# Operand stores on the GpSimd queue, operands made one by one behind weight chunks, and shared loads in the feed-forward part of a transformer block

## Chip, cores and metric

One core of one Trainium2 chip. The metric is the device time of one execution in microseconds (us), lower is better. The kernel before takes 2645.63 us, the median of three runs (2642.18 to 2647.23).

## What is computed

One layer over 512 tokens with 2048 channels, all in float32. The change lies in its second half:

```
z = rms_norm(x) @ w_in                       # then a state-space branch and an attention branch
m = sigmoid(g_s) * (y_ssm @ w_proj_ssm) + sigmoid(g_a) * (y_attn @ w_proj_attn)
x = x + m @ w_out
h = rms_norm(x)
x = x + (silu(h @ w_ffn_gate) * (h @ w_ffn_up)) @ w_ffn_down      # 2048 -> 5632 -> 2048
```

## The kernel before

**Products in float32.** A weight chunk is 128x2x512 (256 rows of the matrix by 512 columns, 512 KB). `split` (L460) makes two parts of it: ScalarE rounds it (`whi`, L461), VectorE takes the rest (`wlo = x - whi`, L462). With an operand that was split in the same way, TensorE does three matmuls: hi by hi, hi by lo, lo by hi. There are three buffers each for `whi` and `wlo`. `linear` (L453) does all matrices up to w_out so.

**The feed-forward part** (`ffn`) uses seven products of half matrices in place of eight. `seven` (L1008 issues its matmuls) goes through the products in the order 1, 2, 7, 5, 6, 3, 4 (in the first unit 1, 7, 2, 5, 6, 3, 4). Each takes its weights chunk by chunk from `weights(i, c)`, then `done(i, banks)` takes the result from PSUM. After each chunk one entry of a list `fill` is run, if any is left.

**Gate and up**: eleven units u = 0 to 10 of 512 hidden columns; in each every product has 4 chunks and 48 matmuls. `weights` sums blocks of the matrices on VectorE (`add`, L1037): A is a slab of 8x512 that goes from w11 to w11-w12 (product 7), then plus w22 (6); product 7 loads two chunks and sums them, 6 and 3 load w22 one after the other, and for product 4 w21 is added to A by an accumulating load on GpSimd's queue (L1108). Raw chunks lie in three buffers and a few places of a slab E.

**Operands of the down product.** When unit u runs, the activations of unit u - 1 are transposed (`flip_act`: four flips of four transposes on TensorE, L1027, evacuated to E by ScalarE, L1060), one behind each chunk of product 2. Behind flip 2 operands 1 and 7 are made, behind flip 4 the other five, each bunch at once: sums on VectorE (L958, L966 to L968), a `split` into two tiles `wk` (L461, L462), and two stores of 256 KB to a buffer `opd` in DRAM on SP's queue (L1066). The pool `wk` has five buffers of 128x512; two of them hold the gate's values from product 1 until product 3 has been evacuated. For unit 0 the operands come out of w_out's result and stay in SBUF; their sums run on GpSimd, in w_out and in unit 0.

**Down**: blocks of units [0], [1, 2], ... [9, 10], each for v = 0 and 1 (two halves of the output). Block 0 has one chunk per product, the others two. Operands come back from `opd` (L1182), product 4 uses an accumulating load again (L1206), and sums stay in SBUF (`done`, L1215 on ScalarE in block 0). The operands of unit 10 are made in block 0, v = 0.

**The end**: `final` (L1155 and on) flips four results, adds x2 (loaded from DRAM to a `wk` tile on ScalarE's queue, L1162) and stores 256 KB (SP, L1164). Eight finals of v = 0 and four of v = 1 are filled into the last block, the last four stand behind it.

**What sets the order.** TensorE's order in `ffn` is that of the program. The other engines' instructions are placed by a scheduler that works from priorities and an estimate of time; each engine then runs its instructions in that fixed order, and one that waits holds all behind it.

Of the kernel before, what the change touches and what calls it, by code (L numbers as in the profile page):

```python
# [12 lines left out]
ALU = mybir.AluOpType  # L13
# [18 lines left out]
class Block:  # L32
# [427 lines left out]
    def split(self, hi, lo, x):  # L460
        self.nc.scalar.activation(hi, x, AF.Copy)  # L461
        self.nc.vector.tensor_tensor(lo, x, hi.bitcast(F32), op=ALU.subtract)  # L462

# [257 lines left out]
    def build(self, out):  # L721
# [226 lines left out]
    ORDER = (1, 2, 7, 5, 6, 3, 4)  # L948
# [32 lines left out]
    def seven(self, n, weights, ops, done, order=ORDER, fill=()):  # L981
# [7 lines left out]
        for i in order:  # L989
            if i in (1, 7):  # L990
                banks[i] = [self.bank("lin") for _ in range(2)]
            elif i in (2, 5):
                banks[i] = [self.bank("S") for _ in range(2)]
            else:
                banks[i] = banks[{6: 1, 3: 5, 4: 7}[i]]
            for c in range(0, n, 2):
                raw = weights(i, c)

                self.nc3 = (self.nc3 + 1) % 3
                hi, lo = (self.wp.tile([P, 2, T], F32R, tag=t, name=self.uid(t)) if self.nc3 else  # L1000
                          self.fp.tile([P, 2, T], F32R, tag=t, name=self.uid(t)) for t in ("whi", "wlo"))
                self.split(hi, lo, raw)
                for kk in range(2):
                    k = c + kk
                    for tt in range(2):
                        xh, xl = (ops[i][:, h, k, tt * P:(tt + 1) * P] for h in range(2))
                        for q, (l, r) in enumerate(((xh, hi), (xh, lo), (xl, hi))):
                            nc.tensor.matmul(banks[i][tt], l, r[:, kk, :], start=(i in (1, 7, 2, 5) and k == 0 and q == 0),  # L1008
                                             stop=(k == n - 1 and q == 2), skip_group_check=True)
                if i != order[0] and fill:  # L1010
                    fill.pop(0)()
            done(i, banks[i])
        assert not fill

# [15 lines left out]
    def ffn(self, ops, steps, x2d, out):  # L1030
# [25 lines left out]
        def flip_act(u, j):  # L1056

            x1, x2 = self.E[:, 4:6], self.E[:, 6:8]
            tp = self.flips([act[u, tt][:, j * P:(j + 1) * P] for tt in range(4)])
            nc.scalar.activation((x1, x2)[j // 2][:, j % 2], tp, AF.Copy)  # L1060
# [7 lines left out]
            if j == 1:  # L1068
                self.operands_1(put, x1, lambda: self.work((P, 2, 256)), dve)
            elif j == 3:  # L1070
                step = self.operands_2(put, x1, x2, dve)
                for i in (2, 5, 6, 3, 4):
                    step(i, 0, True, True)

        flips_act = lambda u: [lambda j=j: flip_act(u, j) for j in range(4)] if u >= 0 else []

        for u in range(NU):
# [4 lines left out]
            def weights(i, c):  # L1082
                for _ in range(2 if i == 7 else 1):
                    if steps:
                        steps.pop(0)()
# [7 lines left out]
                if i in (2, 3):  # L1093
                    return load(raw(), b(2, 1) if i == 2 else b(2, 2))
                if i == 7:
                    r1, r2 = load(raw(), b(1, 2)), load(raw(), b(2, 2))
                    if not first:
                        add(dve, A, A, r1)
                    add(dve, r2, r1, r2)
# [5 lines left out]
                elif i == 6:  # L1105
                    add(dve, A, A, load(raw(), b(2, 2)))
# [40 lines left out]
            order = (1, 7, 2, 5, 6, 3, 4) if first else self.ORDER  # L1147
            self.seven(8, weights, ops, done, order, flips_act(u - 1))
# [7 lines left out]
        def final(v, m, j):  # L1156
# [4 lines left out]
            o = self.work()  # L1161
            nc.scalar.dma_start(o, x2d[t])  # L1162
# [9 lines left out]
        for b, units in enumerate(blocks):  # L1172
# [7 lines left out]
            for i in self.ORDER:  # L1180
                for c, u in enumerate(units):
                    nc.sync.dma_start(ops[i][:, :, 2 * c:2 * c + 2].bitcast(F32), opd[u, i - 1])  # L1182
            for v in range(2):

                o = 2 * v if b == 0 else 0

                def weights(i, c, A=A[:, o:], R=R[:, o:], Q=Q[:, o:]):
# [45 lines left out]
                self.seven(n, weights, ops, done, self.ORDER, fill)  # L1233
                if b or v:
# [41 lines left out]
```

## Time and profile before

| | |
|---|---|
| median of 3 runs | 2645.63 us |
| the profiled execution, and its span | 2639.38 us, 2637.5 us |
| TensorE busy | 2554.5 us (97%) |
| VectorE, ScalarE, GpSimd busy | 2053.7 (78%), 1176.5 (45%), 383.4 us (15%) |
| DMA | 474.28 MB, mean 180 GB/s |
| first matmul of the feed-forward part | at 1280.6 us |
| last matmul of it | ends at 2625.9 us |

Busy time of TensorE counts matmuls at the pace that its clock allowed: after a long wait matmuls are slower and count as busy all the same. So a stage is best read by its length beside that of the same work elsewhere.

### The profile page before, as it was taken

To read this page: it belongs to the slowest core of one execution; us is meant where nothing else is said; L and a number is where in the kernel's file an instruction comes from. 1 tells how busy PE (TensorE), PEld (TensorE's weight loads), DVE (VectorE), ACT (ScalarE), POOL (GpSimd) and SP (SyncE) were. 2 spreads that over 40 slices of the span, in tenths; PEclk is the share of its full clock that TensorE was granted. 3 is DMA by queue.
4 is the path that set the end of the run, shared out by engine and by line. 5 is a ranking of instruction groups with operands and counts; after the bars stand their busy time and mean duration, and the time that the engine had idled before them with its cause. 6 is when DMAs were issued, how large, how long until landed. Compare 5 with 4: busy or idle time off the path is not lost.

```text
span 2637.5 us, 32145 instructions
## 1 busy us (share of the span) xinstructions
PE 2554.5 (97%) x11351; PEld 2043.4 (77%) x11351; DVE 2053.7 (78%) x3345; ACT 1176.5 (45%) x1783; POOL 383.4 (15%) x472
## 2 busy tenths in 40 slices
PE   7999999999999999999999999999999998999998
PEld 5777777777787777888777878887887876888887
DVE  8799999999557865525678887778877786788888
ACT  4244444444255643224444545545545445333332
POOL 5232232221011100015300000000000000000000
PEclk9999999999999999999999999999999998999999
DMA  5444344434443434433668777778777798667774
GB/s 156 144 117 116 113 118 120 122 112 104 124 148 120 133 104 160 156 113 127 200 199 270 220 227 221 221 229 264 218 228 218 230 301 293 188 214 234 242 232 139
DMA packets 243329, 474.28 MB, mean 180 GB/s; under 512 B 22472, under 2 KB 22536, under 8 KB 243168
## 3 DMA queue, kind: packets, MB, share of 16 engines
q1 hardware_dynamic: 201248, 386.98, 45.3%
q0 software_dynamic: 37408, 81.02, 13.4%
q10 hardware_dynamic: 4512, 4.24, 0.6%
q8 instruction: 89, 1.46, 0.2%
q14 instruction: 72, 0.59, 0.1%
HBM read 401.35 MB, written 65.03 MB: 177 GB/s over the span
## 4 chain that ended last, share of the span: by engine, by line
issue 47%; PE 32%; DVE 13%; DMA 3%; POOL 3%; ACT 1%; SPq 0%; DVEq 0%; POOLq 0%; ACTq 0%
PE lin L453 25%; PE lin L1008 3%; PE S L1008 2%; DVE wlo L432 2%; POOL s L1108 2%; DVE c L363 1%; DMA s<-in_w_ffn_down_dram 1%; DVE s L364 1%; PE O L413 1%; DMA bi<-in_ssm_b_im_dram 1%; DVE t L400 1%; DVE wlo L462 1%; DVE t L395 1%; DVE s L1037 1%; POOL s L1206 1%
## 5 line engine op out<-in xcount | busy, mean ns | idle before, releaser
L453 PE MATMUL lin<-s,whi 128*128 128x512 f32 x2432 | 738.6, 396 | 1.6 <-DVE s L462 1.0
L1008 PE MATMUL lin<-whi,s 128*128 128x512 f32 x2112 | 669.8, 393 | 10.0 <-ACT whi L461 10.0
L461 ACT ACTIVATE whi<-s 128x1024 fp32r<-128x1024 f32 x354 | 372.9, 1059 | 459.2 <-PE lin L1008 231.7
L462 DVE TENSOR_TENSOR wlo<-s,whi 128x1024 fp32r<-128x1024 f32 x354 | 431.7, 1223 | 180.4 <-ACT whi L461 179.5
L453 PEld LDWEIGHTS lin<-s,whi 128*128 128x128 f32 x2432 | 453.4, 189 | 124.6 <-issue 22.3
L1008 PE MATMUL S<-whi,s 128*128 128x512 f32 x1584 | 510.0, 393 | 4.0 <-DVE wk L1037 3.4
L1008 PEld LDWEIGHTS lin<-whi,s 128*128 128x128 f32 x2112 | 399.8, 189 | 93.9 <-ACT whi L461 11.3
L453 PE MATMUL lin<-s,wlo 128*128 128x512 f32 x1216 | 448.0, 395 | 12.2 <-DVE wlo L432 12.2
L1008 PE MATMUL lin<-wlo,s 128*128 128x512 f32 x1056 | 417.0, 395 | 22.2 <-DVE wlo L462 22.0
L432 DVE TENSOR_TENSOR wlo<-raw,whi 128x1024 fp32r<-128x1024 f32 (+1 forms) x201 | 252.2, 1255 | 175.3 <-ACT whi L431 168.9
L431 ACT ACTIVATE whi<-raw 128x1024 fp32r<-128x1024 f32 (+1 forms) x201 | 211.3, 1052 | 330.6 <-PE lin L453 283.0
L1008 PEld LDWEIGHTS S<-whi,s 128*128 128x128 f32 x1584 | 298.2, 188 | 66.5 <-ACT whi L461 4.8
L1008 PE MATMUL S<-wlo,s 128*128 128x512 f32 x792 | 309.7, 391 | 4.3 <-DVE wlo L462 4.2
L453 PEld LDWEIGHTS lin<-s,wlo 128*128 128x128 f32 x1216 | 229.8, 190 | 65.9 <-DVE wlo L432 15.5
L1008 PEld LDWEIGHTS lin<-wlo,s 128*128 128x128 f32 x1056 | 200.0, 189 | 74.2 <-DVE wlo L462 33.4
L453 PE MATMUL lin<-whi,s 128*128 128x512 f32 x768 | 245.6, 394 | 0.0
L1008 PEld LDWEIGHTS S<-wlo,s 128*128 128x128 f32 x792 | 149.1, 188 | 36.8 <-DVE wlo L462 6.7
L453 PEld LDWEIGHTS lin<-whi,s 128*128 128x128 f32 x768 | 144.0, 188 | 38.8 <-issue 7.2
L1108 POOL DMA_DIRECT2D s<-in_w_ffn_gate_dram x44 | 53.3, 1223 | 783.7 <-DVE wlo L462 754.6
L462 DVE TENSOR_TENSOR wlo<-raw,whi 128x1024 fp32r<-128x1024 f32 x103 | 125.8, 1225 | 42.5 <-ACT whi L461 42.5
L461 ACT ACTIVATE whi<-raw 128x1024 fp32r<-128x1024 f32 x103 | 108.8, 1057 | 105.8 <-PE S L1008 42.0
L453 PE MATMUL lin<-wlo,s 128*128 128x512 f32 x384 | 150.1, 391 | 2.7 <-DVE wlo L432 2.7
(346 smaller groups left out, 2734.4 us busy)
## 6 DMA issues: line engine op xcount, KB each, us to landing
raw<-in_w_in_dram SPq DMA_DIRECT2D x127, 512.0 KB, 3.8
raw<-in_w_ffn_up_dram SPq DMA_DIRECT2D x115, 512.0 KB, 4.8
opd<-wk SPq DMA_DIRECT2D x154, 256.0 KB, 4.7
s<-opd SPq DMA_DIRECT2D x77, 512.0 KB, 9.0
s<-in_w_ffn_down_dram SPq DMA_DIRECT2D x66, 512.0 KB, 5.8
s<-in_w_ffn_gate_dram SPq DMA_DIRECT2D x64, 512.0 KB, 5.5
s<-in_w_ffn_up_dram SPq DMA_DIRECT2D x60, 512.0 KB, 4.7
s<-in_w_ffn_gate_dram POOLq DMA_DIRECT2D x44, 512.0 KB, 10.5
```

What stands on the lines that cost most here:

```text
L363: nc.vector.scalar_tensor_tensor(c[:, hi], s[:, lo], nps[:, j:j + 1], c[:, hi], op0=ALU.mult, op1=ALU.add)
L364: nc.vector.scalar_tensor_tensor(s[:, hi], c[:, lo], ps[:, j:j + 1], s[:, hi], op0=ALU.mult, op1=ALU.add)
L395: nc.vector.tensor_tensor_scan(t1, mag, t1, 0.0, op0=ALU.mult, op1=ALU.add)
L400: nc.vector.tensor_tensor_scan(t3, mag, t3, 0.0, op0=ALU.mult, op1=ALU.add)
L413: nc.tensor.matmul(y[32 * q:32 * q + 32, :], CT[:, ri, 32 * q:32 * q + 32], states[q][ri], start=(ri == 0), stop=(ri == 1))
L431: nc.scalar.activation(hi[:, ks], raw[:, ks], AF.Copy)
L432: nc.vector.tensor_tensor(lo[:, ks], raw[:, ks], hi[:, ks].bitcast(F32), op=ALU.subtract)
L453: nc.tensor.matmul(acc[b], l, r, start=(k == 0 and i == 0), stop=(k == nk - 1 and i == 2))
L461: self.nc.scalar.activation(hi, x, AF.Copy)
L462: self.nc.vector.tensor_tensor(lo, x, hi.bitcast(F32), op=ALU.subtract)
L1008: nc.tensor.matmul(banks[i][tt], l, r[:, kk, :], start=(i in (1, 7, 2, 5) and k == 0 and q == 0), stop=(k == n - 1 and q == 2), skip_group ...
L1108: pool.dma_start(A, two(b(2, 1)), accum_op=ALU.add)
```

## The change

- Sums of operands of unit 0: from GpSimd to VectorE.
- The order has a group (6, 3): chunk by chunk first 6, then 3, both with one load of w22. Both are evacuated when both are done; product 5, whose banks 3 goes on with, is evacuated before.
- Operands of unit u - 1: flips behind the chunks of product 2 as before, five empty entries, and then one operand each behind chunks 2, 3 and 4 of product 5 and chunks 1 and 2 of 6 and 3. `behind` ties each to the chunk split that goes ahead of it. Sums are made in place. Stores go to GpSimd's queue.
- Block 0 has places of its own for weights, and its product 4 adds on VectorE. Unit 10's operands are spread over both v of block 0.
- x2 of the last eight finals comes by one load of 2 MB into a slab, issued when product 7 of the last v is done.
- In product 7 the sum for r2 comes ahead of that for A; in the first unit the two steps at a time are popped in product 2 in place of 7.

```diff
-        step = self.operands_2(put, x2[0], x2[1], nc.gpsimd)
+        step = self.operands_2(put, x2[0], x2[1], nc.vector)
...
-                    self.operands_1(put, x2[0], lambda: self.work((P, 2, 256)), nc.gpsimd)
+                    self.operands_1(put, x2[0], lambda: self.work((P, 2, 256)), nc.vector)
...
-    ORDER = (1, 2, 7, 5, 6, 3, 4)
+    ORDER = (1, 2, 7, 5, (6, 3), 4)
...
             for c in range(0, n, 2):
-                raw = weights(i, c)
+                for i in group:
+                    raw = weights(i, c)
...
+                    self.last = self.split(hi, lo, raw)
...
+                    if i == group[-1] and c == n - 2:
+                        for j in group:
+                            done(j, banks[j])
+                    if i != order[0] and fill:
+                        fill.pop(0)()
...
+    def behind(self, ins):
+
+        self.tc.add_manual_dep(ins.ins, self.last.ins.name, mybir.DependencyInfo(
+            mybir.DependencyClass.NoSync, mybir.DependencyReason.DATA), reason="order")
...
-            def put(i, k, x):
-                hl = [self.work((P, 2, 256), F32R) for _ in range(2)]
-                self.split(*hl, x)
-                for h in range(2):
-                    nc.sync.dma_start(opd[u, i - 1, :, h], hl[h].bitcast(F32))
...
+            def step(i, x, op=None):
+                def f():
+                    if op:
+                        self.behind(op())
+                    hl = [self.work((P, 2, 256), F32R) for _ in range(2)]
+                    self.behind(self.split(*hl, x))
+                    for h in range(2):
+                        pool.dma_start(opd[u, i - 1, :, h], hl[h].bitcast(F32))
+                return f
...
+            return [step(1, x11), step(2, x12),
+                    step(7, x11, lambda: add(dve, x11, x11, x21, ALU.subtract)),
+                    step(5, x21, lambda: add(dve, x21, x21, x22, ALU.subtract)),
+                    step(6, x11, lambda: dve.scalar_tensor_tensor(x11, x11, -1.0, x22, op0=ALU.mult, op1=ALU.subtract)),
+                    step(3, x12, lambda: add(dve, x12, x12, x11)),
+                    step(4, x22)]
...
-                for _ in range(2 if i == 7 else 1):
+                for _ in range(2 if i == 2 else 1):
...
+                if i == 3:
+                    return st["w22"]
                 if i == 7:
                     r1, r2 = load(raw(), b(1, 2)), load(raw(), b(2, 2))
+                    add(dve, r2, r1, r2)
                     if not first:
                         add(dve, A, A, r1)
-                    add(dve, r2, r1, r2)
...
                 elif i == 6:
-                    add(dve, A, A, load(raw(), b(2, 2)))
+                    st["w22"] = load(raw(), b(2, 2))
+                    add(dve, A, A, st["w22"])
...
-            self.seven(8, weights, ops, done, order, flips_act(u - 1))
+            self.seven(8, weights, ops, done, order, flips_act(u - 1) + [lambda: None] * 5 + make(u - 1) if u else ())
...
-            o = self.work()
-            nc.scalar.dma_start(o, x2d[t])
+            if v:
+                o = st["x2"][:, t - 8]
+            else:
+                o = self.work()
+                nc.scalar.dma_start(o, x2d[t])
...
+                    own = self.A[:, 6 * v:], raw() if v else self.A[:, 2:], self.A[:, 4:]
...
                     if i == 4:
-                        pool.dma_start(A, two(blk(2, 1)), accum_op=ALU.add)
+                        if n == 2:
+                            add(dve, A, A, R)
+                        else:
+                            pool.dma_start(A, two(blk(2, 1)), accum_op=ALU.add)
...
+                    if last and v and i == 7:
+
+                        st["x2"] = self.slab("s7", (P, 8, T), F32)
+                        nc.sync.dma_start(st["x2"], x2d[8:16].rearrange("k p t -> p k t"))
...
                 if b == 0 and v == 0:
-                    fill = both(flips_act(NU - 1))
+                    made = make(NU - 1)
+                    fill = both(flips_act(NU - 1)) + made[:4]
+                elif b == 0:
+                    fill = made[4:]
```

How this moves instructions shows at three places. In the names, `s_1872` is A; E is `s_1899` before and `s_1907` after; `lin` and `S` are PSUM banks.

**VectorE in product 7 of unit 1, before.** L1037 are sums of weights or evacuations, L958, L966 and L967 sums of operands, `wk` the low halves of operands.

```order
L462 TENSOR_TENSOR wlo_11957<-raw_11952,whi_11956 128x1024
L1037 TENSOR_TENSOR wk_11777<-wk_11777,S_11781 128x512
L1037 TENSOR_TENSOR s_1872_11382<-s_1872_11382,s_1899_11549 128x1024
L1037 TENSOR_TENSOR s_1899_11549<-s_1899_11549 128x1024
L1037 TENSOR_TENSOR wk_11779<-wk_11779,S_11782 128x512
L462 TENSOR_TENSOR wlo_11979<-raw_11974,whi_11978 128x1024
L966 TENSOR_TENSOR s_1899_11549<-s_1899_11549 128x2x256
L462 TENSOR_TENSOR wk_11838<-wk_11835,wk_11837 128x512
L462 TENSOR_TENSOR wlo_11999<-s_1899_11549,whi_11998 128x1024
L967 TENSOR_TENSOR s_1899_11549<-s_1899_11549 128x2x256
L462 TENSOR_TENSOR wlo_12017<-s_1872_11382,whi_12016 128x1024
```

**VectorE from the end of product 7 of unit 1 on, after the change.** The first row splits the last chunk of product 7, the next the first chunk of 5.

```order
L462 TENSOR_TENSOR wlo_11946<-raw_11941,whi_11945 128x1024
L462 TENSOR_TENSOR wlo_11964<-s_1872_11382,whi_11963 128x1024
L1048 TENSOR_TENSOR s_1872_11382<-s_1872_11382,raw_12052 128x1024
L462 TENSOR_TENSOR wlo_11980<-s_1872_11382,whi_11979 128x1024
L462 TENSOR_TENSOR wk_11996<-s_1907_11613,wk_11995 128x512
L1048 TENSOR_TENSOR s_1872_11382<-s_1872_11382,raw_12101 128x1024
L462 TENSOR_TENSOR wlo_12002<-s_1872_11382,whi_12001 128x1024
L462 TENSOR_TENSOR wk_12018<-s_1907_11613,wk_12017 128x512
L1048 TENSOR_TENSOR s_1907_11613<-s_1907_11613 128x2x256
L1048 TENSOR_TENSOR s_1872_11382<-s_1872_11382,s_1907_11613 128x1024
L462 TENSOR_TENSOR wlo_12024<-s_1872_11382,whi_12023 128x1024
L462 TENSOR_TENSOR wk_12047<-s_1907_11613,wk_12046 128x512
```

Operand work is no longer between the splits of product 7; a half (later with a sum ahead of it) now stands behind each split of 5, 6 and 3.

**SP's queue in unit 1, before**, where stores of operands stand among the loads of weights:

```order
L1066 DMA opd<-wk_11892 128x512
L1066 DMA opd<-wk_11898 128x512
L1053 DMA raw_12184<-in_w_ffn_up_dram 128x2x512
L1066 DMA opd<-wk_11905 128x512
L1066 DMA opd<-wk_11899 128x512
L1053 DMA raw_12202<-in_w_ffn_up_dram 128x2x512
L1066 DMA opd<-wk_11912 128x512
L1066 DMA opd<-wk_11906 128x512
```

**GpSimd's queue in unit 1, after the change** (L1086 are the stores, L1132 the accumulating loads of product 4; before, those loads stood alone here):

```order
L1086 DMA opd<-wk_12072 128x512
L1132 DMA s_1872_11382<-in_w_ffn_gate_dram 128x2x512
L1086 DMA opd<-wk_12073 128x512
L1086 DMA opd<-wk_12095 128x512
L1086 DMA opd<-wk_12096 128x512
L1086 DMA opd<-wk_12121 128x512
L1132 DMA s_1872_11382<-in_w_ffn_gate_dram 128x2x512
L1086 DMA opd<-wk_12122 128x512
L1086 DMA opd<-wk_12143 128x512
L1132 DMA s_1872_11382<-in_w_ffn_gate_dram 128x2x512
L1086 DMA opd<-wk_12144 128x512
L1132 DMA s_1872_11382<-in_w_ffn_gate_dram 128x2x512
```

The stores of 154 tiles leave SP's queue, and four of a unit's stores now follow its first accumulating load.

**VectorE in block 0, v = 0, after the change**, from the split for product 5 (first row) over those for 6 and 3 to the one for product 4 (last row):

```order
L462 TENSOR_TENSOR wlo_17844<-s_1872_11382,whi_17843 128x1024
L1048 TENSOR_TENSOR s_1872_11382<-s_1872_11382 128x1024
L462 TENSOR_TENSOR wk_17862<-s_1907_11613,wk_17861 128x512
L1048 TENSOR_TENSOR s_1907_11613<-s_1907_11613 128x2x256
L462 TENSOR_TENSOR wlo_17869<-s_1872_11382,whi_17868 128x1024
L1048 TENSOR_TENSOR s_1872_11382<-s_1872_11382 128x1024
L462 TENSOR_TENSOR wlo_17893<-s_1872_11382,whi_17892 128x1024
L1048 TENSOR_TENSOR s_1907_11613<-s_1907_11613 128x2x256
L462 TENSOR_TENSOR wk_17887<-s_1907_11613,wk_17886 128x512
L462 TENSOR_TENSOR wlo_17919<-s_1872_11382,whi_17918 128x1024
```

The sixth row is the sum that takes the place of the accumulating load, ahead of the splits for products 3 and 4; halves and sums of unit 10's operands (`wk`, `s_1907`) stand between them.

## Rows read from the trace of the kernel before

**Rows 1.** The page's first part: busy us, share of the span and number of instructions of each engine.

```profile
PE 2554.5 (97%) x11351; PEld 2043.4 (77%) x11351; DVE 2053.7 (78%) x3345; ACT 1176.5 (45%) x1783; POOL 383.4 (15%) x472
```

**Rows 2.** The view of the waits of TensorE over the whole span: what waited, for what, us in total, times, longest.

```profile
PE lin L1008 <- DVE wlo L462: 22.0, 21, 3.4
...
PE lin L1008 <- ACT whi L461: 10.0, 3, 5.8
...
PE S L1008 <- DVE wk L1037: 3.4, 1, 3.4
```

**Rows 3.** Windows of the span: start and end in us, length, busy us (and instructions) of TensorE, its weight loads, VectorE, ScalarE and GpSimd, granted clock, share of the DMA engines, GB/s. In order: 66 us of w_out; unit 0; units 1 to 10; of unit 2 products 2, 7, 6 and 4; of unit 10 product 3; block 0 with v = 0 and v = 1; from the last product's end to the span's end.

```profile
1188.00:1254.00 66.00, 66.00 (x293) 54.66 (x292) 39.45 (x28) 27.60 (x37) 34.44 (x26) 1.00 0.39 125
1280.60:1372.20 91.60, 81.70 (x345) 65.88 (x344) 73.54 (x83) 46.62 (x59) 23.73 (x18) 0.96 0.81 250
1372.20:2173.50 801.30, 786.62 (x3521) 644.85 (x3521) 628.07 (x651) 408.64 (x490) 48.42 (x40) 1.00 0.78 234
1463.50:1476.20 12.70, 12.70 (x66) 10.47 (x64) 11.06 (x11) 6.90 (x10) 0.00 (x0) 1.00 0.78 236
1476.20:1488.40 12.20, 11.40 (x52) 9.07 (x50) 10.92 (x13) 7.00 (x9) 0.00 (x0) 1.00 0.90 300
1499.20:1510.70 11.50, 11.19 (x50) 8.93 (x48) 9.45 (x10) 6.57 (x9) 4.85 (x4) 1.00 1.06 264
1521.60:1532.50 10.90, 10.90 (x50) 9.03 (x49) 8.57 (x10) 4.25 (x4) 0.00 (x0) 1.00 0.61 203
2147.60:2160.50 12.90, 11.52 (x50) 9.02 (x49) 5.94 (x7) 6.36 (x8) 0.00 (x0) 1.00 1.06 309
2173.50:2201.20 27.70, 23.98 (x102) 19.09 (x101) 21.41 (x26) 18.94 (x30) 1.20 (x1) 0.89 0.61 184
2201.20:2231.90 30.70, 22.84 (x85) 17.52 (x84) 17.68 (x17) 14.33 (x20) 1.20 (x1) 0.83 1.03 352
2626.00:2637.50 11.50, 3.33 (x24) 2.25 (x22) 4.52 (x7) 0.00 (x0) 0.00 (x0) 0.75 0.60 205
```

**Rows 4.** Timeline of VectorE in product 7 of unit 2: start in us, us, engine, line, operation, output and inputs, then the idle time before it and what ended it.

```profile
1478.80 1.23 DVE L1037 TENSOR_TENSOR s<-s,s 128x1024 f32<-128x1024 f32 x1 [1.28 <-DMA s<-in_w_ffn_up_dram]
...
1481.67 1.22 DVE L462 TENSOR_TENSOR wlo<-raw,whi 128x1024 fp32r<-128x1024 f32 x1
1482.81 0.69 DVE L966 TENSOR_TENSOR s<-s 128x512 f32<-128x512 f32 x1
1483.41 0.69 DVE L462 TENSOR_TENSOR wk<-wk,wk 128x512 fp32r<-128x512 f32 x1
1484.01 1.22 DVE L462 TENSOR_TENSOR wlo<-s,whi 128x1024 fp32r<-128x1024 f32 x1
```

**Rows 5.** Timeline of ScalarE shortly after.

```profile
1489.00 0.64 ACT L461 ACTIVATE wk<-s 128x512 fp32r<-128x512 f32 x1 [2.12 <-DMA opd<-wk]
```

**Rows 6.** The view of the tensor opd: who waited for it (us, times).

```profile
  ACT wk L461: 55.6, 29
```

**Rows 7.** The view of the DMA issues by group: names, queue, count, KB each, median us from issue to landing.

```profile
opd<-wk SPq DMA_DIRECT2D x154, 256.0 KB, 4.7
...
s<-in_w_ffn_gate_dram POOLq DMA_DIRECT2D x44, 512.0 KB, 10.5
...
x2d<-s POOLq DMA_DIRECT2D x16, 256.0 KB, 2.5
...
out_dram<-wk SPq DMA_DIRECT2D x16, 256.0 KB, 2.7
```

**Rows 8.** Groups of GpSimd's instructions by line: count, busy us, mean ns of one.

```profile
L966 POOL TENSOR_TENSOR s<-s,s 128x512 f32<-128x512 f32 x4 | 7.0, 1754 | 4.6 <-ACT s L909 4.6
```

**Rows 9.** Timeline of VectorE in unit 0.

```profile
1292.54 1.75 DVE L462 TENSOR_TENSOR s<-s,s 128x512 fp32r<-128x512 f32 x1
...
1295.35 2.28 DVE L462 TENSOR_TENSOR wlo<-ring,whi 128x1024 fp32r<-128x1024 f32 x1
```

**Rows 10.** Timeline of TensorE in unit 0, the first matmul after a wait and one 3.07 us later.

```profile
1297.69 0.79 PE L1008 MATMUL lin<-wlo,s 128*128 128x512 f32 x1 [3.37 <-DVE wlo L462]
...
1300.76 0.63 PE L1008 MATMUL lin<-whi,s 128*128 128x512 f32 x2
```

**Rows 11.** Timeline of ScalarE in block 0.

```profile
2193.94 1.06 ACT L461 ACTIVATE whi<-s 128x1024 fp32r<-128x1024 f32 x1 [4.88 <-DMA s<-in_w_ffn_down_dram]
...
2210.75 1.06 ACT L461 ACTIVATE whi<-s 128x1024 fp32r<-128x1024 f32 x1 [3.87 <-DMA wk<-x2d]
...
2224.68 2.00 ACT L461 ACTIVATE whi<-s 128x1024 fp32r<-128x1024 f32 x2 [3.16 <-DMA s<-in_w_ffn_down_dram]
```

**Rows 12.** Timeline of TensorE in block 0.

```profile
2195.05 0.79 PE L1008 MATMUL lin<-whi,s 128*128 128x512 f32 x1 [3.25 <-ACT whi L461]
...
2225.79 0.79 PE L1008 MATMUL lin<-whi,s 128*128 128x512 f32 x1 [5.85 <-ACT whi L461]
...
2227.64 1.05 PE L1008 MATMUL lin<-whi,s 128*128 128x512 f32 x2
...
2228.92 1.05 PE L1008 MATMUL lin<-whi,s 128*128 128x512 f32 x2
```

**Rows 13.** Timeline of VectorE at the end.

```profile
2633.72 0.69 DVE L1037 TENSOR_TENSOR wk<-wk,T 128x512 f32<-128x512 f32 x1 [3.58 <-DMA wk<-x2d]
```

**Rows 14.** The view of line L1108, the accumulating loads of the units.

```profile
DMA to landing us min/median/max: 6.7/10.5/16.1
```

More of the change, by code (lines that the diff above doesn't have):

```diff
@@ L988, in seven @@
         fill = list(fill)
[L989 to L995, printed above, removed]
-            for c in range(0, n, 2):
-                raw = weights(i, c)
[L999 to L1012, printed above, removed]
@@ new lines, in seven @@
+        for group in order:
+            group = group if isinstance(group, tuple) else (group,)
+            for i in group:
+                if i in (1, 7):
+                    banks[i] = [self.bank("lin") for _ in range(2)]
+                elif i in (2, 5):
+                    banks[i] = [self.bank("S") for _ in range(2)]
+                else:
+                    banks[i] = banks[{6: 1, 3: 5, 4: 7}[i]]
+            for c in range(0, n, 2):
+                for i in group:
+                    raw = weights(i, c)
+                    self.nc3 = (self.nc3 + 1) % 3
+                    hi, lo = (self.wp.tile([P, 2, T], F32R, tag=t, name=self.uid(t)) if self.nc3 else
+                              self.fp.tile([P, 2, T], F32R, tag=t, name=self.uid(t)) for t in ("whi", "wlo"))
+                    self.last = self.split(hi, lo, raw)
+                    for kk in range(2):
+                        k = c + kk
+                        for tt in range(2):
+                            xh, xl = (ops[i][:, h, k, tt * P:(tt + 1) * P] for h in range(2))
+                            for q, (l, r) in enumerate(((xh, hi), (xh, lo), (xl, hi))):
+                                nc.tensor.matmul(banks[i][tt], l, r[:, kk, :], skip_group_check=True,
+                                                 start=(i in (1, 7, 2, 5) and k == 0 and q == 0), stop=(k == n - 1 and q == 2))
+                    if i == group[-1] and c == n - 2:
[3 more added lines that the diff above has]
+                        fill.pop(0)()
@@ L1056, in flip_act, with make @@
         def flip_act(u, j):
+            tp = self.flips([act[u, tt][:, j * P:(j + 1) * P] for tt in range(4)])
+            nc.scalar.activation(self.E[:, 4 + j], tp, AF.Copy)
+        flips_act = lambda u: [lambda j=j: flip_act(u, j) for j in range(4)]
+        def make(u):
             x1, x2 = self.E[:, 4:6], self.E[:, 6:8]
-            tp = self.flips([act[u, tt][:, j * P:(j + 1) * P] for tt in range(4)])
-            nc.scalar.activation((x1, x2)[j // 2][:, j % 2], tp, AF.Copy)
-            def put(i, k, x):
-                hl = [self.work((P, 2, 256), F32R) for _ in range(2)]
-                self.split(*hl, x)
-                for h in range(2):
-                    nc.sync.dma_start(opd[u, i - 1, :, h], hl[h].bitcast(F32))
[L1068 to L1075, printed above, removed]
+            a, b = slice(0, 256), slice(256, 512)
+            def step(i, x, op=None):
[7 more added lines that the diff above has]
+                return f
+            x11, x21, x12, x22 = x1[:, :, a], x1[:, :, b], x2[:, :, a], x2[:, :, b]
+            return [step(1, x11), step(2, x12),
[4 more added lines that the diff above has]
+                    step(4, x22)]
         for u in range(NU):
@@ L1179, in ffn @@
                     ops[i] = t[:, h]
-            for i in self.ORDER:
+            for i in (1, 2, 7, 5, 6, 3, 4):
                 for c, u in enumerate(units):
@@ L1183, in ffn, with weights @@
             for v in range(2):
-                o = 2 * v if b == 0 else 0
-                def weights(i, c, A=A[:, o:], R=R[:, o:], Q=Q[:, o:]):
+                st = {}
+                if b == 0:
+                    own = self.A[:, 6 * v:], raw() if v else self.A[:, 2:], self.A[:, 4:]
+                else:
+                    own = A, R, Q
+                def weights(i, c, A=own[0], R=own[1], Q=own[2]):
                     r0 = 4 * units[c // 2]
```

14 lines of the change are left out of this document (8 added, 6 removed).

## The prediction

> **What bounds the kernel now.** I read the page's busy shares first: TensorE is busy for 97% of the span, VectorE for 78% [rows 1]. So nearly everything is at TensorE's own pace, and the only time to be had is what TensorE loses. The view of what TensorE waited for says to whom: in the feed-forward part (line L1008) 22.0 us to VectorE's low halves of weights, 10.0 us to ScalarE's high halves, 3.4 us to VectorE's evacuations [rows 2]. That view leaves out the slow clock after a wait, so I cut the span into stages and compared each with the pace of an unhindered product [rows 3]: product 4 of unit 2 takes 10.9 us for its 48 matmuls (0.227 us each), product 2 with its four flips 12.7. A unit without loss is therefore 6 x 10.9 + 12.7 = 78.1 us. Losses by stage:
>
> - Unit 0: 91.6 - 7 x 10.9 = 15.3 us.
> - Units 1 to 10: 801.3 - 10 x 78.1 = 20.3 us.
> - Short block (block 0): 27.7 + 30.7 = 58.4 us for 168 matmuls (38.1) and four flips (1.8): 18.5 us lost, with a granted clock of 0.89 and 0.83.
> - Behind the last product: 11.5 us, of which TensorE works 3.3.
>
> The change can win some 60 us at the very most, and every part of it aims at one of these places.
>
> **Units 1 to 10.** In product 7 of unit 2 (12.2 us, so 1.3 lost) VectorE also makes operands: between the weight split at 1481.67 and the one at 1484.01 stand a sum and the low half of another operand [rows 4]. One of 128x512 costs 0.60 us from start to start (1482.81 to 1483.41), a weight split 1.14 (1481.67 to 1482.81); product 7 also has two sums of weights per chunk at 1.22 each. Beside that ScalarE stands still until an operand's store has freed a buffer: 2.12 us at 1489.00 [rows 5]; these waits sum to 55.6 us in 29 places [rows 6]. The change takes all operand work out of product 7 and puts one operand behind one chunk of products 5, 6 and 3. It does not take work away: VectorE still has the same sums and halves. In the first two pairs of 6 and 3 a pair of chunks asks of VectorE one sum of weights (1.14), two splits (2.28) and two operands with their sums (4 x 0.60): 5.8 us where TensorE needs 5.4; the last two pairs need 3.4 and catch up. Three buffers of split weights cover a lag of 0.4 to 0.8 us, and the evacuation of product 5 on top (two of 0.60) as well, just. I leave 0.5 us per unit as lost: gain 20.3 - 5 = 15. At best all 20; at worst none, or a loss, below.
>
> The four loads of w22 that 6 and 3 now share take 2 MB out of each unit. They cost VectorE and TensorE nothing before, since raw loads were waited for in only one place: product 3 of unit 10, 12.9 us for 10.9 [rows 3]; those 2.0 us are in the 20.3. Evacuating 5 before 3 begins (it shares its banks) asks two ScalarE copies within 2.72 us where there were 13.6; copies are short beside that, so I cost it at nothing while ScalarE isn't held by a store.
>
> The stores now stand on GpSimd's queue, between the accumulating loads of product 4. A store of 256 KB took a median 4.7 us on SP's queue, 2.5 on GpSimd's (x2d); an accumulating load took 10.5 [rows 7]. No row of before has a store behind such a load. Of wk's five buffers two hold the gate's values up to product 3, so a tile waits for the store of the tile three before it, some 1.5 steps or 4.1 us earlier: 2.5 fits, 4.7 is late by less than the cover. I take 2.5, the same size on the same queue. For this the Trainium skill has a warning (SBUF — State Buffer, section on SBUF's two separate sides): a DMA of the GpSimd queue needs descriptors written by GpSimd, which a VectorE instruction in a two-port mode locks out. By it stores on this queue land later the busier VectorE is, and the sum would move towards the time of the third rival. The trace agrees with it only in that the accumulating loads, of the same queue, are slow; the x2d stores at 2.5 us, beside a VectorE busy 39.45 of 66 us [rows 3], speak against it, and no row shows which instructions run in that mode.
>
> **Unit 0.** GpSimd's sums of operands move to VectorE. On GpSimd one of L966 took 1.75 us [rows 8]; on VectorE such a sum is 0.60. Beside GpSimd's arithmetic VectorE's own operations stretched: a 128x512 half took 1.75 us at 1292.54, a weight split 2.28 at 1295.35, in place of 0.68 and 1.22 [rows 9]. TensorE then stood 3.37 us at 1297.69, and eight matmuls up to 1300.76 took 3.07 us instead of 1.82 [rows 10]: 4.6 us together. I take 5 as gained. What is left is loads and the evacuation of product 2 (3.4 [rows 2]), which the change puts behind one more sum. Bounds: 0, if VectorE is late anyway with 6 sums more, and 10 of the 15.3.
>
> **The short block.** Product 4's weights came by an accumulating load: ScalarE waited 4.88 us for one at 2193.94 and 3.16 at 2224.68 [rows 11]; TensorE stood 3.25 and 5.85 us, and then went at 1.28 us per three matmuls (2227.64 to 2228.92), the level of 1.2 GHz, for twelve of them: 12 x (0.427 - 0.227) = 2.4 us each time [rows 12]. Sum 9.1 + 4.8 = 13.9. In their place stands one VectorE sum of 1.22 each. Its cover is thin: VectorE's 21.4 + 17.7 = 39.1 busy us plus 2.4 are as long as TensorE's 40, and ScalarE is held here by loads of x2 into wk, 3.87 us at 2210.75 [rows 11], which now wait for the stores on the other queue. The second v moves 352 GB/s [rows 3], 10.8 MB in 30.7 us, much of it operands for block 1; if it gets shorter, those loads are waited for in block 1. Gain 13, of which 2 come back: 11; bounds 4 (one wait gone, the rest turned into others) and 18.5.
>
> **The end.** The last final waited 3.58 us at 2633.72 for its x2 [rows 13], which waited for a buffer of wk. Now all eight lie in a slab. The outer store (2.7 us [rows 7]) stays. Gain 3.5, bounds 2 and 5.
>
> **w_out.** GpSimd's other ten sums fall in a stretch where TensorE is at 66.00 of 66 us and VectorE at 39.45 [rows 3]: nothing, covered by 26 us of free VectorE.
>
> **Sum.** 15 + 5 + 11 + 3.5 = 34.5 us. The profiled execution took 2639.4, so 2604.9; it lies 6.2 under the median of 2645.6, which is the scale I forecast on: 2645.6 - 34.5 = 2611. With single bounds moved (units 20, block 17, unit 0 9, end 4) 2596; with units 8, unit 0 at 2, block 4, end 2 it is 2630. A measurement of this kernel tells some 0.2%, 5.3 us, from no change.
>
> **Rivals.** *Units gain nothing.* Product 7 of unit 2 moved 300 GB/s where the ten units have a mean of 234 [rows 3], and VectorE waited 1.28 us there for a weight [rows 4]. If product 7 is late for its two loads per chunk, spreading operands helps nothing: 19.5 us gained, 2626. For it: that wait; against it: the 22.0 us of rows 2 are put down to VectorE, and ScalarE's waits to stores. The Trainium skill (DMA: Bandwidth & Descriptors, section Issuing engines are not separate DMA queues) says that all issuers feed the same 16 engines and another one saves only issuing time; by it alone the move of the stores gives nothing, and the gain hangs on the spreading. *The short block only swaps waits*: 4 instead of 11, 2618; its row for this is the thin cover above. *Slower: stores wait behind the accumulating load of their own queue.* Four of a unit's stores follow the first accumulating load directly, and if the ring serves them in order, they land after 10.5 + 2.5 = 13.0 us. Covered are 4.1 us by buffers and two chunks (5.4) by split weights, so ScalarE and then TensorE stand 3.5 us, and lose 1.3 more at the low clock [rows 10]: 4.8 a unit, 48 in all, where 20.3 are lost now: 28 us slower, less 19.5 from the other places: 2654. It turns slower when a store so placed lands over 12 us after the load's issue. For it: the accumulating loads reach 16.1 us at most [rows 14]; against it: all four of a unit were issued within product 6, beside a DMA share of 1.06 [rows 3], and now they come one per pair of chunks. The skill's page on DMA (Two DMAs through the same engine are not ordered) says descriptors of one queue start in order, which is this rival's condition but not its price.
>
> **Chances.** Forecast as worked out 0.60; units gain nothing 0.15; short block alone fails 0.12; stores behind the load 0.10; a sum of several small failures that leaves no change 0.03. The range reaches from 2595 to 2633, which takes in the first three and leaves out the slower one and the full bounds. Faster 0.86, same 0.05, slower 0.09.
>
> **What would show it.** Right: units of 78 to 79 us with product 7 at 10.9; no wait of ScalarE for opd stores above 1 us; stores on the GpSimd queue at 3 us; block 0 at 43 to 48 us with a clock near 1; under 8.5 us behind the last product. Wrong: waits of TensorE in 6 and 3 that end with a half of wk or of its neighbours, or units of 80 and more.

## The result

The changed kernel takes 2612.72 us (median of 4 runs, 2609.8 to 2614.05), the one before 2646.16 beside it: a ratio of 0.9875, with a 95% interval of 0.9858 to 0.9892. A second time, on another chip, it was 0.9892 (0.9875 to 0.9908). By the medians it is 33 and 31 us faster; 2611 had been forecast. The profiled execution took 2609.8 us against 2639.4, 29.6 less; the profile of before lies 7 us under its median, this one 3, so the parts below, read from the two profiles, sum to some 29.5 and not to 33.

The page of the changed kernel, TensorE and VectorE; TensorE is at 98% [rows 1]:

```profile
PE 2549.0 (98%) x11351; PEld 2041.7 (78%) x11351; DVE 2053.4 (79%) x3363; ACT 1176.4 (45%) x1783; POOL 436.8 (17%) x608
```

What its TensorE waited for (L1012 is L1008 of before):

```profile
PE lin L1012 <- DVE wlo L462: 12.2, 13, 2.8
...
PE lin L1012 <- ACT whi L461: 0.8, 2, 0.6
```

These were 22.0 and 10.0 us [rows 2]; the wait for evacuations has left the list. Its windows by stage, columns as in rows 3: w_out's end, unit 0, units 1 to 10, product 7 of unit 2, block 0 in two rows, block 1 with v = 0, and what is behind the last product:

```profile
1215.00:1282.10 67.10, 67.10 (x297) 55.58 (x296) 30.32 (x32) 22.38 (x29) 8.49 (x9) 1.00 0.36 114
1282.10:1367.40 85.30, 80.31 (x345) 64.86 (x344) 71.90 (x89) 46.90 (x58) 12.37 (x12) 0.98 0.79 243
1367.40:2157.10 789.70, 785.43 (x3522) 645.26 (x3521) 628.05 (x651) 409.94 (x490) 126.97 (x180) 1.00 0.70 211
1470.70:1482.10 11.40, 11.35 (x52) 9.06 (x51) 10.96 (x12) 6.28 (x8) 0.57 (x1) 1.00 0.79 256
2157.10:2177.90 20.80, 20.80 (x102) 17.38 (x101) 19.18 (x23) 17.71 (x28) 4.35 (x8) 1.00 0.45 152
2177.90:2199.30 21.40, 19.68 (x86) 15.55 (x84) 15.01 (x17) 12.49 (x20) 3.23 (x6) 1.00 0.93 333
2199.30:2245.50 46.20, 40.87 (x168) 32.60 (x169) 35.02 (x36) 17.43 (x19) 2.44 (x2) 0.96 0.82 273
2599.80:2608.00 8.20, 3.33 (x24) 2.25 (x22) 4.44 (x7) 0.00 (x0) 0.00 (x0) 0.89 0.51 192
```

| stage, us | before | after | difference | forecast |
|---|---|---|---|---|
| up to the feed-forward part | 1280.6 | 1282.1 | +1.5 | 0 |
| unit 0 | 91.6 | 85.3 | -6.3 | -5 |
| units 1 to 10 | 801.3 | 789.7 | -11.6 | -15 |
| block 0 | 58.4 | 42.2 | -16.2 | -13 |
| block 1, v = 0 | 38.4 | 46.2 | +7.8 | +2 |
| the rest up to the last product | 355.6 | 354.3 | -1.3 | 0 |
| behind it | 11.5 | 8.2 | -3.3 | -3.5 |

The 1.5 us at the front arise in the first 130 us, which the change doesn't touch (w_out runs at TensorE's pace in both).

### The profile page after: what moved, and what is told of

It is laid out like the page before. It is cut to its first block, busy times and chain, and to the rows that moved or that the text cites. A ratio compares the mean times of both kernels' runs of the same rounds, so it can differ in the third digit from the quotient of the medians.

```text
span 2608.0 us, 32145 instructions
## 1 busy us (share of the span) xinstructions
PE 2549.0 (98%) x11351; PEld 2041.7 (78%) x11351; DVE 2053.4 (79%) x3363; ACT 1176.4 (45%) x1783; POOL 436.8 (17%) x608
## 4 chain that ended last, share of the span: by engine, by line
PE 45%; issue 31%; DVE 14%; DMA 5%; POOL 3%; ACT 1%; DVEq 0%; POOLq 0%; ACTq 0%; SPq 0%
PE lin L453 25%; PE lin L1012 10%; PE S L1012 7%; DVE wlo L432 2%; DMA raw<-in_w_ffn_up_dram 2%; DVE wlo L462 1%; DMA s<-in_w_ffn_up_dram 1%; POOL opd L1086 1%; POOL s L1240 1%; DVE c L363 1%; DVE s L364 1%; PE O L413 1%; DMA bi<-in_ssm_b_im_dram 1%; DVE t L395 1%; DVE t L400 1%
## 5 line engine op out<-in xcount | busy, mean ns | idle before, releaser
L1012 PE MATMUL lin<-whi,s 128*128 128x512 f32 x2112 | 672.8, 392 | 0.8 <-ACT whi L461 0.8
L1012 PE MATMUL S<-whi,s 128*128 128x512 f32 x1584 | 514.2, 392 | 2.6 <-DVE rs L93 1.6
L1012 PEld LDWEIGHTS lin<-whi,s 128*128 128x128 f32 x2112 | 398.1, 188 | 83.9 <-ACT whi L461 1.6
L1012 PE MATMUL lin<-wlo,s 128*128 128x512 f32 x1056 | 414.9, 393 | 12.3 <-DVE wlo L462 12.2
L1012 PEld LDWEIGHTS S<-whi,s 128*128 128x128 f32 x1584 | 297.4, 188 | 64.6 <-ACT whi L461 3.4
L1012 PE MATMUL S<-wlo,s 128*128 128x512 f32 x792 | 309.2, 390 | 4.4 <-DVE wlo L462 4.4
L1012 PEld LDWEIGHTS lin<-wlo,s 128*128 128x128 f32 x1056 | 199.0, 188 | 61.5 <-DVE wlo L462 20.9
L1086 POOL DMA_DIRECT2D opd<-wk x154 | 90.1, 594 | 677.6 <-ACT wk L461 602.3
L1012 PEld LDWEIGHTS S<-wlo,s 128*128 128x128 f32 x792 | 148.9, 188 | 37.1 <-DVE wlo L462 7.4
```

The source lines that it names most:

```text
L1012: nc.tensor.matmul(banks[i][tt], l, r[:, kk, :], skip_group_check=True, start=(i in (1, 7, 2, 5) and k == 0 and q == 0), stop=(k == n - 1 ...
L1086: pool.dma_start(opd[u, i - 1, :, h], hl[h].bitcast(F32))
```

## Experiments

All start from the changed kernel. "Units" is the time of units 1 to 10 in the profiled execution (789.7; 788.5 when it was profiled again).

**1. The stores back on SP's queue.**

```diff
-                        pool.dma_start(opd[u, i - 1, :, h], hl[h].bitcast(F32))
+                        nc.sync.dma_start(opd[u, i - 1, :, h], hl[h].bitcast(F32))
```

> The changed kernel with the operand stores back on SP's queue; operands are still made one behind each chunk of products 5, 6 and 3. Theory A (the spreading is what freed product 7, the queue is worth little): units 1 to 10 take 789.7 us as in the changed kernel, give or take 3, and the time is 2610 to 2617. Rival B (the queue itself matters, since a store that waits for its half holds the weight loads behind it on SP): weight loads come late in products 6 and 3, units 1 to 10 grow by 6 to 15 us and the time is 2619 to 2628. Rival C (stores behind the accumulating load of the same queue cost something now, 62 of 142 stores land only after it): without that ScalarE and VectorE wait less for stores and units shrink by 2 to 4 us.

Measured: units 790.1, median 2604.1, ratio 0.9863 (0.9849 to 0.9878). Theory A holds for the units, B and C don't: the move to GpSimd's queue gave nothing there, though the waits for stores are shorter on SP's, 41 us for 61. The median lies 6 us under A's range, with an interval that overlaps the changed kernel's. Between the two profiles 3 of the 6 us arise ahead of the feed-forward part, the other 3 in block 1 with v = 0, which takes 43.4 us for 46.2:

```profile
2195.80:2239.20 43.40, 40.33 (x170) 32.52 (x169) 32.47 (x34) 17.02 (x19) 2.41 (x2) 0.96 0.93 306
```

**2. Operands in bunches again**, behind flips 2 and 4.

```diff
+        def bunch(u):
+            f, s = flips_act(u), make(u)
+            return [f[0], lambda: (f[1](), s[0](), s[2]()), f[2], lambda: (f[3](), s[1](), s[3](), s[4](), s[5](), s[6]())]
...
-            self.seven(8, weights, ops, done, order, flips_act(u - 1) + [lambda: None] * 5 + make(u - 1) if u else ())
+            self.seven(8, weights, ops, done, order, bunch(u - 1) if u else ())
```

In `step` the two calls of `behind` go, so nothing is tied to a chunk.

> The changed kernel with all operands of a unit made in product 2 again (1 and 7 behind flip 2, the other five behind flip 4, nothing tied to a chunk); the stores stay on GpSimd's queue. Theory A (spreading): product 7 loses 1.3 to 2.2 us per unit again, units 1 to 10 go from 789.7 to some 798 to 802 us, the time to 2621 to 2625. Rival B (the queue): units stay at 790, time 2613.

Measured: units 808.4, 2622.8 us. Theory A holds for the direction and the time, but the units are 6 us past its bound: product 7 takes 11.3 to 14.8 us and loses 22.1 us over ten units (16.7 before the change), and products 5, 6 and 3 lose 6.3.

**3. The same with stores on SP's queue**, the edits of 1 and 2 together.

> Operands in two bunches in product 2, stores on SP's queue, loads of w22 still shared. With the stores on GpSimd's queue the bunches gave 808.4 us for units 1 to 10; the kernel before, on SP and without sharing, 801.3. Theory (in a bunch no accumulating load is ahead of most stores, what counts is VectorE's work in product 7, and sharing does nothing for it): 799 to 803. Rival (the sharing alone frees product 7): under 795.

Measured: units 803.6, 2619.4 us in one run. The theory missed its bound by 0.6; the rival is out: sharing without the spreading frees nothing, product 7 still loses 17.5 us.

**4. Product 3 loads w22 itself.**

```diff
                 if i == 3:
-                    return st["w22"]
+                    return load(raw(), b(2, 2))
```

> The changed kernel, but product 3 loads w22 itself instead of using the load of product 6; their order stays interleaved. Theory A (raw loads bound nothing in 6 and 3 but for unit 10): units 1 to 10 within 2 us of 789.7, of which unit 10 alone takes up to 2. Rival: the load on the DMA engines counts (2 MB more in each unit, and the accumulating loads run in the same stretch), units 1 to 10 grow by 4 to 8 us, and accumulating loads go from a median of 8.1 us back towards 10.5.

Measured: units 806.4, 2625.7 us in one run. Theory A is wrong, and the rival's size too small. The loss is in products 6 and 3 (15.8 us over ten units), the accumulating loads hardly changed (median 8.5). Who waited for the stores (the view of line L1086), first in the changed kernel:

```profile
who waited for it (us, times):
  DVE wk L462: 36.1, 23
  ACT wk L461: 25.3, 15
...
DMA to landing us min/median/max: 2.3/4.1/10.5
```

and with separate loads:

```profile
  ACT wk L461: 56.4, 21
  DVE wk L462: 48.0, 30
...
DMA to landing us min/median/max: 2.3/5.2/10.7
```

The stores land 1.1 us later, past the 4.1 us that wk's three free buffers cover, and the waits for them go from 61 to 104 us. Such a wait reaches TensorE over VectorE. In unit 4 the half of an operand waits for a store, the split of the next chunk stands behind it, and TensorE waits for that split:

```profile
1668.05 0.69 DVE L462 TENSOR_TENSOR wk<-s,wk 128x512 fp32r<-128x512 f32 x1 [2.57 <-DMA opd<-wk]
1668.66 1.22 DVE L462 TENSOR_TENSOR wlo<-raw,whi 128x1024 fp32r<-128x1024 f32 x1
...
1669.93 0.50 PE L1012 MATMUL S<-wlo,s 128*128 128x512 f32 x1 [1.17 <-DVE wlo L462]
```

Followed back in this way, 16 of TensorE's 20 waits of over 0.1 us in products 6 and 3 begin at a store that had not landed, and none at a load of weights (the other four chains are too long to follow). In the changed kernel there is one such wait.

**5. Separate loads and stores on SP's queue**, the edits of 1 and 4 together.

> Product 3 loads w22 itself again and the stores are on SP's queue. With the stores on GpSimd's queue the separate loads cost 16.7 us in units 1 to 10 (806.4). Theory H (the extra loads make the accumulating loads slower, and stores behind them in the same queue then hold the wk buffers): on SP the stores land sooner, units come back to 790 to 794. Rival I (stores land late under the larger load on whichever queue): units stay at 800 to 808.

Measured: units 810.2, 2622.7 us in one run; 2 us past the bound of rival I; stores land after a median of 5.4 us on SP's queue too, and 21 of 22 waits in 6 and 3 begin at one. Rival I holds in that it is not the queue. The DMA share in the units is 0.78, where the changed kernel has 0.70; that this larger load makes the stores late is its reading, not shown apart from the places that the extra loads take.

**6. Product 2 evacuated one split later.**

```diff
+            def evac2():
+                for tt in range(2):
+                    g = st["g", tt]
+                    self.after_lo(add(dve, g, g, st["late"][tt]))
+                    nc.scalar.activation(g, g, AF.Silu, scale=self.r2[:, tt:tt + 1])
...
-            self.seven(8, weights, ops, done, order, flips_act(u - 1) + [lambda: None] * 5 + make(u - 1) if u else ())
+            self.seven(8, weights, ops, done, order, flips_act(u - 1) + [lambda: None] * 2 + [evac2] + [lambda: None] * 2 + make(u - 1) if u else ())
```

`after_lo` ties an instruction behind VectorE's last split, and `done` leaves product 2 to `evac2`.

> The changed kernel with one thing moved: in units 1 to 10 VectorE evacuates product 2 behind its split of the third chunk of product 7 (it now runs ahead of that split). Theory D (what product 7 still loses, 8.5 us over ten units, is VectorE's order: evacuation and sum stand ahead of the split that TensorE waits for): the third chunk of product 7 takes 2.72 to 3.0 us instead of 2.96 to 4.28, units 1 to 10 take 782 to 785 us, the time is 2605 to 2608. Rival E (the loads of product 7 land late, so the split moves with them): the wait stays where it is, units at 788 to 790 and the time at 2612.

What it rests on is VectorE's timeline in product 7 of unit 1 of the changed kernel: behind the sum for the third chunk (1393.51) come the sum for A, the evacuation, and only then the split (1396.98) that TensorE waits for until 1398.26.

```profile
1393.51 1.23 DVE L1048 TENSOR_TENSOR raw<-s,raw 128x1024 f32<-128x1024 f32 x1 [1.44 <-DMA s<-in_w_ffn_up_dram]
1394.65 1.22 DVE L1048 TENSOR_TENSOR s<-s,s 128x1024 f32<-128x1024 f32 x1
1395.79 1.28 DVE L1048 TENSOR_TENSOR wk<-wk,S 128x512 f32<-128x512 f32 x2
1396.98 1.22 DVE L462 TENSOR_TENSOR wlo<-s,whi 128x1024 fp32r<-128x1024 f32 x1
```

Measured: 2608.3 us, 0.9881 (0.9864 to 0.9897), units 788.4. Product 7's loss over ten units fell from 8.5 to 3.6 us as theory D says, but 6 and 3 lost 4.9 in place of 1.1. Theory D is right on the wait and wrong on the units, E the other way round: VectorE's order in product 7 was a cause of that wait, though it begins at a late load (1.44 us in the first row), and the work put off there is late in 6.

**7. x2 of v = 0 loaded late.**

```diff
-                nc.scalar.dma_start(o, x2d[t])
+                self.behind(nc.scalar.dma_start(o, x2d[t]))
```

> The changed kernel with the eight loads of x2 for the finals of v = 0 tied behind the chunk splits of the last block (five of them now stand in ScalarE's queue in block 0, among its evacuations and splits). In the changed kernel the first v of block 1 takes 46.3 us where 38.1 are its pace, and ScalarE stood 4.68 and 3.78 us there behind two of these loads until a load of operands landed. Theory F (ScalarE, held by the issue of these loads, makes block 1 late): block 1 with v = 0 takes 40 to 43 us, the time falls by 3 to 6 us. Rival G (operands and weights are late by themselves: 388 GB/s at a DMA share of 1.05): it stays within 2 us of 46.3 and the time within 2 us.

The changed kernel's ScalarE in block 1, two of its rows; the loads of x2 (ACTq) stand in its queue just ahead of each:

```profile
2196.80 0.33 ACTq L1189 DMA_DIRECT2D wk<-x2d  x1
2197.17 1.09 ACT L1253 ACTIVATE s<-lin 128x512 f32<-128x512 f32 x2 [4.68 <-DMA s<-opd]
...
2204.53 0.33 ACTq L1189 DMA_DIRECT2D wk<-x2d  x1
2204.91 1.09 ACT L1253 ACTIVATE s<-lin 128x512 f32<-128x512 f32 x2 [3.78 <-DMA s<-opd]
```

Windows of the experiment, block 0 and block 1 with v = 0:

```profile
2159.80:2203.90 44.10, 42.16 (x186) 34.20 (x185) 37.61 (x41) 33.32 (x50) 7.58 (x14) 0.96 0.66 232
2203.90:2242.00 38.10, 38.10 (x170) 31.52 (x169) 30.95 (x33) 15.32 (x16) 2.48 (x2) 1.00 0.90 297
```

Theory F holds for the place: block 1 takes 38.1 us at TensorE's pace, though the loads of operands are the same; rival G is out. Block 0 gives 1.9 of the 8.1 us back. The time, 2607.4 us and 0.9851 (0.9823 to 0.9879), doesn't separate it from the changed kernel on another chip; 9 does.

**8. Block 0, the tail and unit 0, one undone in each kernel.** Block 0 with the accumulating load:

```diff
-                        if n == 2:
-                            add(dve, A, A, R)
-                        else:
-                            pool.dma_start(A, two(blk(2, 1)), accum_op=ALU.add)
+                        pool.dma_start(A, two(blk(2, 1)), accum_op=ALU.add)
```

> The changed kernel with product 4 of block 0 made by the accumulating load again. Theory (the two waits were worth 13 to 16 us in block 0, but the loads for block 1 lose that time): block 0 goes from 42.2 to 54 to 58 us, block 1 with v = 0 from 46.3 back to 38 to 40, so the time is only 5 to 9 us longer. Rival (block 1's loss has its own cause): block 1 stays at 45 or more and the time is 13 to 16 us longer.

Measured, one run: block 0 60.1 us, block 1 with v = 0 38.5, 2620.8 us. The theory holds for the trade, with block 0 2 us past its bound and 10 us net in the two stages instead of 5 to 9. (The loads of x2 are issued by 2205.7 here, in the longer block 0, so they hold nothing in block 1.)

```profile
2156.60:2216.70 60.10, 44.04 (x186) 34.75 (x186) 36.67 (x40) 32.70 (x50) 10.06 (x16) 0.89 0.83 271
2216.70:2255.20 38.50, 38.50 (x170) 31.83 (x169) 29.52 (x31) 15.35 (x15) 2.44 (x2) 0.99 0.66 198
```

The last finals' x2 through wk:

```diff
-            if v:
-                o = st["x2"][:, t - 8]
-            else:
-                o = self.work()
-                nc.scalar.dma_start(o, x2d[t])
+            o = self.work()
+            nc.scalar.dma_start(o, x2d[t])
```

(and the load of 2 MB in `done` goes).

> The changed kernel with x2 of the last eight finals loaded one by one into wk on ScalarE's queue, as before. Theory: what follows the last product goes from 8.2 back to 11 to 12 us, nothing else moves. Rival (the tail is shorter for another reason, the order of the finals): it stays below 9.

Measured, one run: 10.8 us behind the last product, 0.2 short of the theory's 11, and 2614.9 us in all. VectorE waits there again as in rows 13:

```profile
2609.47 0.69 DVE L1048 TENSOR_TENSOR wk<-wk,T 128x512 f32<-128x512 f32 x1 [2.99 <-DMA wk<-x2d]
```

Unit 0's sums on GpSimd:

```diff
-        step = self.operands_2(put, x2[0], x2[1], nc.vector)
+        step = self.operands_2(put, x2[0], x2[1], nc.gpsimd)
```

(and the same for `operands_1`).

> The changed kernel with the sums of unit 0's operands on GpSimd again. Theory: unit 0 goes from 85.3 to 89 to 92 us, with the 128x1024 split stretched to over 2 us beside GpSimd's sums. Rival (unit 0 gained by popping two steps in product 2 in place of 7 and by the order of the sums): it stays at 85 to 87.

Measured, one run: unit 0 92.5 us, 2619.1 us in all; the theory holds, to 0.5 us past its bound, and the stretched split is back:

```profile
1295.97 2.28 DVE L462 TENSOR_TENSOR wlo<-ring,whi 128x1024 fp32r<-128x1024 f32 x1
```

**9. The changed kernel beside a faster one**, with the edits of 1 and 7.

> The changed kernel itself, timed on the same chip as the three beside it. All theories: a ratio of 0.987 to 0.989 to the kernel before, units 1 to 10 at 788 to 792 us.

> The changed kernel with two edits together: stores on SP's queue, and the loads of x2 for v = 0 tied behind the last block's splits. Theory (the GpSimd queue is worth nothing to the stores, and the x2 loads in ScalarE's queue cost block 1 some 6 us): units stay at 788 to 792, block 0 with block 1's first v takes 82 to 84 us instead of 88.5, the time is 6 to 9 us below the changed kernel's on this chip. Rival (the gain of each was chance between runs): within 2 us of the changed kernel.

Measured: the changed kernel 2612.3 us, 0.9892; with both edits 2603.6 us, 0.9858 (0.9843 to 0.9872), so 8.7 us less by the medians. The two profiles: units 788.5 and 790.3; block 0 with block 1's v = 0 91.2 and 81.6. Time and place are as the theory says, and the rival is out. How the 8.7 us divide between the two edits is not shown: these two blocks take 85.3 us with the first edit alone (1) and 82.2 with the second alone (7). The windows of the kernel with both, units 1 to 10, block 0, block 1 with v = 0:

```profile
1365.70:2156.00 790.30, 784.55 (x3521) 645.39 (x3520) 629.28 (x651) 410.85 (x490) 48.14 (x40) 1.00 0.70 211
2156.00:2197.90 41.90, 40.36 (x186) 33.12 (x185) 37.50 (x41) 32.87 (x50) 0.00 (x0) 1.00 0.68 232
2197.90:2237.60 39.70, 38.70 (x170) 31.37 (x169) 31.29 (x34) 15.21 (x16) 2.41 (x2) 1.00 0.91 299
```

By the medians it is the fastest of all that ran, but the runs don't tell it from 1 (2604.1 us) or 7 (0.9851), which ran on other chips.

## Why the prediction was right, and where not

The time was right, and so was the way in most places; two terms were wrong in cause or size, and one reading of the rows. That the median came within 2 us of 2611 is in part luck: between the two profiles the gain is 29.5 us for 34.5. The units gave 3.4 less than forecast and block 1 took 5.8 more, and block 0 (3.2) and unit 0 (1.3) made up part of it.

Of the signs that I had named, the units (78.5 to 79.7 us), block 0 (42.2, at a clock of 1.00) and the end (8.2) came. Three did not: product 7 took 11.0 to 12.6 us instead of 10.9, the stores 4.1 us instead of 3, and ScalarE waited over 1 us for a store ten times, at most 3.97.

**Units.** The gain came, 11.6 us (12.8 in the second profile) for 15. The 0.5 us per unit that I left as lost in 6 and 3 were in product 7, which still loses 8.5 us of 16.7, where 6 and 3 lose 1.1. My reading of rows 4 was wrong: the operand's sum and half at 1482.81 and 1483.41, which I took for the delay, stand behind the split that TensorE waited for. These are the two rows of VectorE that rows 4 leave out, and TensorE's wait:

```profile
1479.94 1.22 DVE L1037 TENSOR_TENSOR s<-s 128x1024 f32<-128x1024 f32 x1
1481.08 0.68 DVE L1037 TENSOR_TENSOR wk<-wk,S 128x512 f32<-128x512 f32 x1
...
1482.95 0.50 PE L1008 MATMUL lin<-wlo,s 128*128 128x512 f32 x1 [0.80 <-DVE wlo L462]
```

The wait begins at a load of weights, for which VectorE stood 1.28 us; two sums of weights, an evacuation and the split follow, and no work on operands. Followed back so, nine of the ten waits of before in product 7, all at its third chunk, begin at such a load, landed 4.9 to 6.1 us after its issue. In the changed kernel seven do, with 3.7 to 4.8 us. So the first rival had its condition, two loads that come late. The spreading helped all the same, since bunches cost 13.5 us on SP's queue and 18.7 on GpSimd's; by which way it reaches product 7 is not shown. Experiment 6 shows that this can't simply be ordered away. Counted with the durations of rows 4, VectorE has from product 7 to the second pair of 6 and 3 four times 3.4 us, 1.2 for product 2, 4.6 and 2.4 in product 5, 11.6 and 1.2 behind it: 34.7 us where TensorE has 32.6. What is put off in one product is late in the next.

**The step that failed is the shared load, costed at nothing.** I had argued that raw loads were waited for in one place only. Six kernels tell the parts apart:

| units 1 to 10, us | w22 loaded twice | w22 shared |
|---|---|---|
| operands in bunches | 801.3 (before: on SP, 6 and 3 one after the other) | 808.4, on SP 803.6 |
| operands one by one | 806.4, on SP 810.2 | 789.7, on SP 790.1 |

Neither part alone gains anything; both together do. That 6 and 3 alternate is common to all cells but that of before, and no run undoes it alone. Spread operands need each store to land before the buffers come round, 4.1 us by my own count, and 2 MB of loads per unit less bring the median store there (4.1 for 5.2). The sharing paid through the stores, not through the weights: that is where the waits of experiments 4 and 5 begin. Their sum doesn't measure the loss, though: 104 us of waits for stores go with 15.8 lost in 6 and 3, 83 on SP's queue with 19.5, 61 in the changed kernel with 1.1. That the DMA share is the cause, and not the places the extra loads take, is argued and not shown.

**Stores on GpSimd's queue.** I took 2.5 us, as x2d's stores took. The third rival's condition was real: the trace, issue by issue, has 62 stores of the units issued while an accumulating load was under way, and all 62 landed after it, by 0.6 to 3.5 us; their median is 6.2 us, that of the other 78 is 2.3. But the load itself lands after 8.1 us in place of 10.5 [rows 7], and counted from the issue of the load just ahead the stores land after 8.7 us by the median; one of the 62 is past the 12 from which I had it decide (12.1). So the mechanism was there and its price covered in the units. By the Trainium skill's rule that issuers share the same engines (DMA: Bandwidth & Descriptors, Issuing engines are not separate DMA queues) the move gives nothing, and experiment 1 agrees in the units: 790.1 on SP's queue, 789.7 on GpSimd's. The Trainium skill's warning on VectorE and descriptors (SBUF — State Buffer, SBUF: two separate sides) is on a two-port mode, not on a busy VectorE as I applied it, and it didn't show: the 78 stores took 2.3 us beside a VectorE busy 628 of 790 us.

**Unit 0.** 6.3 for 5, and 7.2 when undone: the sums' place is the cause.

**Blocks 0 and 1.** The wait and the slow clock went as worked out (16.2 for 13). What came back in block 1 was mis-sized, 7.8 us for 2, and for another cause than the one I gave. I had the loads of x2 as an item of block 0 and loads of operands as block 1's limit; experiment 7 shows that the x2 loads in ScalarE's queue were it: their issue waits until a load of operands has landed, and evacuations and splits stand behind. The operands come in time once ScalarE is free, with 297 GB/s moved in all. The stores' queue has a part in it: in experiment 1 ScalarE stands 1.8 us at an x2 load, for a store, in place of 4.68 and 3.78 for operands. Six profiles with operands one by one, x2 loaded early and stores on GpSimd's queue have 44.4 to 47.9 us in this stage, the two on SP's queue 43.4 and 40.6 (1 and 5). By these profiles the move to GpSimd's queue cost some 3 us here; why a load of operands holds the x2 load is open.

**The end** came as worked out: 3.3 for 3.5, and 2.6 when undone.

With either half of the change left out the first rival's result (units gain nothing) would have come: 803.6 to 810.2 us where before has 801.3.

## What to carry to other kernels

Ask of each transfer that is dropped which other transfers it lets land sooner, and whether a ring of buffers waits for those; here stores that landed 1.1 us later by the median went with 17 us. What stands next to a wait need not be its cause: follow the wait back to what released it. Two parts of a change can be worth nothing alone and 12 us together, so undo them in pairs. A prefetch in the queue of an engine that computes is an instruction that can wait: tie it behind the work that must not stand behind it.

## What had not been expected of the hardware

Stores issued behind an accumulating load on GpSimd's queue never landed ahead of it (62 of 62 in both profiles of the changed kernel). On SP's queue (1) 30 of the 70 stores issued while such a load was under way landed ahead of it. The accumulating loads of the units took a median of 8.1 and 7.7 us in the two profiles of the changed kernel, and 9.6 in both kernels whose operands were also made one by one with shared loads but stored on SP's queue (1 and 9); why is open, and the units were no longer for it.
